# Two-layer hybrid trunk: sums of squares taken where the latents leave PSUM, negations on another engine, corner products as a stream of their own

## The chip, the cores and the metric

One core of a Trainium2 chip runs the whole program, in one launch. The metric is the device time of one execution in microseconds (us). Before the change the median of three runs is 3110.48 us (3110.13 to 3112.98).

## What is computed

Two identical layers over 1024 tokens of width 1024, all in float32. Each layer is a mixer block and a convolutional feed-forward block, each with a norm before and after. In the mixer one projection feeds four head groups:

```python
h = rms_norm(x, pre_mix_norm[l]); p = h @ w_in[l]
pa, pb, pc, pd = split_last(p, [A_COLS, B_COLS, C_COLS, D_COLS])
o = concat([mla_mixer(pa), gqa_mixer(pb), mamba2_mixer(pc), deltanet_mixer(pd)])
x = x + rms_norm(o @ w_out[l])
x = x + rms_norm(conv_ffn(rms_norm(x)))
```

Two parts matter here. Group A is latent attention: its 352 columns are a query latent of 192, a key-value latent of 128 and 32 rotary columns. Each latent is RMS-normalised over its own columns and then projected up to queries, keys and values, so each token needs two sums of squares. Group D is a gated delta rule in chunks of 64 tokens: for every chunk and head a unit lower-triangular 64 x 64 matrix is inverted. Its two 32 x 32 diagonal blocks are inverted first, and the corner of the inverse is made of products of the inverted blocks with the 32 x 32 block off the diagonal.

## The kernel before

The engines are TensorE (PE), VectorE (DVE), ScalarE (ACT), GpSimd (POOL) and SyncE (SP), which issues nearly all DMAs. Each runs its own instructions in a fixed order and stops at the first one whose input is missing. A layer runs through three stages. In the first, `step_a` (L567) projects the columns of group A, one of eight 128-token tiles at a time; the helper at L570 copies the result out of PSUM on ACT (L572), has POOL pick out gate columns (L573) and stores 352 columns to DRAM (`pa_d`). The second, the mixing stage, does everything between the projection and the output projection. The third is the output projection and the feed-forward, long runs of full-size matmuls.

The mixing stage is the one the change touches. It is written as streams, Python generators of which each step emits the instructions of one piece of work:

- `nats` (L578): projections of token-major columns. Its matmuls are L552. Columns of z leave PSUM by a tanh on ACT (L591, into a ring of three tiles `pb`) and a multiply on DVE (L592, that frees the PSUM tile); columns of group B by a copy on ACT (L586).
- `prep_a` (L1303): loads the latents back from `pa_d` twice. The first pass (L1326 to L1329) loads eight tiles through two buffers and takes the squares on ACT with an accumulated sum; DVE makes the reciprocal roots (`rstd`, L156 to L165). The second pass, per tile, loads again (L1338), transposes on PE (L1342 to L1344), splits into two parts (`lh`, ACT L133 and DVE L135), projects (L1350, L1351 for queries, L1354 for keys and values), copies out with the reciprocal root as scale (ACT L1356, L1358, L1359), rotates on POOL and stores to `qa_d` and `ka_d` (L1366, L1367).
- `d_inverse` (L910): loads the off-diagonal blocks (`ni`), negates them on ACT (L927 for one half of the partitions, read transposed, and L928 for the other), POOL copies pieces (L931), DVE inverts by 15 substitution steps (L937, L938) and block products (L946, L947). The result goes through DRAM (`u_d`, `x_d`), and `Xi` and `NX` are loaded back with 32 x 32 blocks on the partitions (L974, L975). Then the corner: 128 matmuls of 32 x 32 (L988), in eight PSUM tiles, and two copies to `Et` on ACT for each tile (L990).
- `mixer_c` (L749): the state-space mixer of group C. Its chunk states are L796 (from `X`, `bt` and `cz`), its later matmuls L825, L833, L839 and L853, some of them in the same two-buffer PSUM pool (`p1`) as the corner.
- `att` (L1371, L1122): group A's attention and then group B's. It loads one head's keys from `ka_d` (`kn`, L1395), transposes them (L507), does the same for queries (`qn`, L1388), then scores (L1139), exponentials on ACT (L1147), transposes (L507) and products with the values (L1174).
- `mixer_d` (L994): the recurrence of group D; it reads `Et` in L1034.

The order is set in two steps. A table `when` (L439) gives each stream a start and an end on an arbitrary scale, and `weave` (L1405) divides the span by the number of steps given in `mix` (L1427) and always advances the stream whose next due time is smallest. That fixes the order in which the program is written and so its priorities; the framework's scheduler then arranges the instructions of each engine by its own estimate of the timeline. Two asserts keep `mixer_d` behind the corner and attention behind `prep_a`.

Of the kernel before, what the change touches and what calls it, by code (L numbers as in the profile page):

```python
# [10 lines left out]
F32 = mybir.dt.float32  # L11
F32R = mybir.dt.float32r
I32 = mybir.dt.int32
BF16 = mybir.dt.bfloat16
AF = mybir.ActivationFunctionType
ALU = mybir.AluOpType
# [4 lines left out]
EPS = 1e-6  # L21
# [403 lines left out]
def ring(make, n):  # L425
    tiles, k = [], [0]

    def get():
        if len(tiles) < n:
            tiles.append(make())  # L430
        k[0] += 1
        return tiles[(k[0] - 1) % n]

    return get


class Mix(Trunk):
    deep = dict(y=2, th=2, sT=1, nat=2, K=1, qn=1, p=2, WO=3)
    when = dict(T=(0, 11, 0), nats=(8.58, 18.19, -719), d_prep=(6.5, 7.0, 0),  # L439
                d_inverse=(11.23, 17.34, 0), mixer_c=(16.33, 24.6, 0), prep_a=(13.24, 18.6, 0),  # L440
                att=(19.5, 47.52, 0), mixer_d=(23.21, 43.4, 0), prep_b=(22.4, 32.29, 141))
    gate_cols = (IN_DT, 8), (IN_AB, 16)
    par_at = 2
# [111 lines left out]
    def begin(self, l, P, between=None):  # L555
        w = P["w_in"][l]
        dram = lambda n, s: self.dr.tile(s, F32, name=self.nm(n), tag=n)
        self.pa_d, self.pb_d, self.z_d = dram("pa_d", [L, 352]), dram("pb_d", [L, 512]), dram("z_d", [L, 512])
        self.k_d, self.v_d, self.qT_d = dram("k_d", [L, 256]), dram("v_d", [L, 256]), dram("qT_d", [2, 4, 64, L])
        self.xs_d, self.bn_d, self.bt_d = dram("xs_d", [L, 256]), dram("bn_d", [L, 128]), dram("bt_d", [128, L])  # L560
        self.ct_d = dram("ct_d", [8, 128, 2, 128])
        self.gin = self.par([128, 8, 24], "gin")
        self.wA = self.nat_load(w, IN_A, 352, self.gate_cols, between=between)
        self.kT, self.qT = [None, None], [None, None]
        self.done = set()

    def step_a(self, i):  # L567
        nc = self.nc

        def evac(i, po):  # L570
            e = self.s2([128, 512], nm="pa")
            nc.scalar.activation(out=e[:, :376], in_=po, func=AF.Copy)  # L572
            nc.gpsimd.tensor_copy(self.gin[:, i, :], e[:, 352:376])  # L573
            nc.sync.dma_start(self.pa_d[i * 128:(i + 1) * 128, :], e[:, :352])

        self.nat_step(self.wA, i, evac)
# [333 lines left out]
    def d_inverse(self):  # L910
        nc = self.nc
        v, g = nc.vector, nc.gpsimd
# [10 lines left out]
        for b in range(2):  # L923
            ni = self.s4([128, 32, 32], nm="ni")
            nc.sync.dma_start(ni, niv[:, b, :, b, :])
            n = self.s4([128, 32, 32], nm="nn")
            nc.scalar.activation(out=n[0:64], in_=ni[0:64].rearrange("p j i -> p i j"), func=AF.Copy, scale=-1.0)  # L927
            nc.scalar.activation(out=n[64:128], in_=ni[64:128], func=AF.Copy, scale=-1.0)  # L928
            for e in range(2):
                h = slice(16 * e, 16 * e + 16)  # L930
                g.tensor_copy(nd[:, b, e], n[:, h, h])  # L931
            nn.append(n)
# [24 lines left out]
        X, T = [nd[:, b, 0] for b in range(2)], [nd[:, b, 1] for b in range(2)]  # L957
# [12 lines left out]
        NX, X = self.s4([128, 8, 4, 32], nm="NX"), self.s4([128, 8, 4, 32], nm="Xi")  # L970
        for d in range(2):
            for cc in range(2):
                o = cc * 64 + d * 32
                nc.sync.dma_start(NX[o:o + 32], self.ni_d[d, :, :, cc, d * 32:d * 32 + 32, (1 - d) * 32:(1 - d) * 32 + 32].rearrange("t h j i -> j (t h) i"))  # L974
                nc.sync.dma_start(X[o:o + 32], self.x_d[d, :, :, cc].rearrange("t h j i -> j t h i"))  # L975
        self.Et = []
        for tp in range(4):
            if tp % 2 == 0:
# [15 lines left out]
    def mixer_d(self, o_d):  # L994
        nc = self.nc
        v, g = nc.vector, nc.gpsimd
# [16 lines left out]
        def load(s):  # L1013
            wo, km, kn = rW(), rK(), rKn()
            flat = lambda ap: ap.rearrange("p h c -> p (h c)")
            for d, t, cc in place(s):
                o = t * 128 + cc * 64
                b, ra, rb, oc = own(d)
                g.memset(wo[rb, 0, d, :, d * 32:d * 32 + 32], 0.0)
                for e in range(2):  # L1020
                    nc.sync.dma_start(wo[b + e * 32:b + 32 + e * 32, 0, d, :, e * 32:e * 32 + 32], self.u_d[d, t, :, cc, e].rearrange("h j i -> j h i"))
                nc.sync.dma_start(flat(kn[tok[d]]), self.k_d[o:o + 64, :])
                nc.sync.dma_start(flat(km[tok[d], 1, d]), self.v_d[o:o + 64, :])
                nc.sync.dma_start(wo[sta[d], 1, d], self.qT_d[d, :, :, o:o + 64].rearrange("h c i -> c h i"))
                nc.sync.dma_start(flat(wo[tok[d], 1, d]), self.q_d[d, t, cc * 64:cc * 64 + 64, :])
            return wo, km, kn
# [40 lines left out]
                for t in (s // 2, (15 - s) // 2):  # L1067
                    self.d_out(t, Od[t // 4][:, t % 4], o_d)

        assert "d_inverse" in self.done  # L1070
        q = [load(0)]
        for d in range(2):
            g.memset(q[0][1][sta[d], 1, d], 0.0)
# [229 lines left out]
    def prep_a(self, l, P):  # L1303
        nc = self.nc
        v, g = nc.vector, nc.gpsimd
# [11 lines left out]
        wkv = self.s4([128, 2, 512], F32R, "wukv")  # L1317
        nc.scalar.activation(out=wkv[:, 0, :], in_=raw, func=AF.Copy, scale=self.gcol[:, 2:3])
        v.scalar_tensor_tensor(wkv[:, 1, :], raw, self.gcol[:, 2:3], wkv[:, 0, :].bitcast(F32), op0=ALU.mult, op1=ALU.subtract)
        ssq, ssk = self.t(self.sml, [128, 8], F32, "ss8"), self.t(self.sml, [128, 8], F32, "ss8")  # L1320
        rSrc, rL, rQK = (ring(lambda nm=nm, dt=dt: self.s2([128, 384], dt, nm), n) for nm, dt, n in (("pa", F32, 2), ("lh", F32R, 4), ("qa", F32, 4)))
        rJ, rTmp = ring(lambda: self.s1([128, 256]), 2), ring(lambda: self.s1([128, 4, 32]), 4)
        for t in range(8):
            junk = rJ()
            src = rSrc()[:, :352]
            nc.sync.dma_start(src, self.pa_d[t * 128:(t + 1) * 128, :])  # L1326
            nc.scalar.activation(out=junk[:, :192], in_=src[:, 0:192], func=AF.Square, accum_out=ssq[:, t:t + 1])
            junk = rJ()
            nc.scalar.activation(out=junk[:, :128], in_=src[:, 192:320], func=AF.Square, accum_out=ssk[:, t:t + 1])  # L1329
        rq = self.rstd(ssq, 1.0 / 192, EPS, 8)  # L1330
        rk = self.rstd(ssk, 1.0 / 128, EPS, 8)
        v.tensor_scalar(rq, rq, 96 ** -0.5, None, op0=ALU.mult)
        VA = []
        qa_d = self.dr.tile([L, 4, 96], F32, name=self.nm("qa_d"), tag="qa_d")
# [1 line left out]
        for t in range(8):  # L1336
            src = rSrc()[:, :352]
# [19 lines left out]
            k = rQK().rearrange("p (h c) -> p h c", h=4)  # L1357
# [69 lines left out]
    def mix(self, l, P, o_d, tail):  # L1427
        first = self.load_T(*self.T_jobs(l, P)[0][:2])
        self.params_ready()
        self.gates()  # L1430
        self.gains_ready()
        att = self.chain(self.attend_a(o_d), self.attend_b(tail))
        self.weave(T=(self.run_T(self.T_jobs(l, P), first, self.nc.gpsimd, True), 11), nats=(self.nats(l, P), 33), d_prep=(self.d_prep(), 8),
                   d_inverse=(self.d_inverse(), 25), mixer_c=(self.mixer_c(o_d), 17), prep_a=(self.prep_a(l, P), 8),
                   att=(att, 70), mixer_d=(self.mixer_d(o_d), 34), prep_b=(self.prep_b(l, P), 6))

    def out_proj(self, l, P, o_d, *tail):
# [143 lines left out]
```

## Time and profile before

| | us |
|---|---|
| median of three runs | 3110.48 |
| the profiled execution | 3117.32 |
| its span, first to last instruction | 3115.5 |
| PE busy | 2980.0 (96%) |
| DVE busy | 1814.4 (58%) |
| ACT busy | 1232.6 (40%) |
| POOL busy | 700.4 (22%) |

The profile is of one execution. Times in it are microseconds from the start of the span. "Idle before" is the time for which an engine had nothing running before an instruction, and behind the arrow stands what came last of the things it waited for. "PEclk" is the clock that TensorE was granted, as a share of 2.4 GHz; it has two levels, 1.00 and 0.50. A float32 matmul is recorded as more than one instruction, so a count of records is not a count of calls: one call of the corner product leaves two records.

### The profile page before, as it was taken

The page shows a single profiled execution, that of the slowest core. Times are in us where ns is not written, and L with a number is a line of the kernel's source. Part 1 is how long each engine was busy: PE and PEld are TensorE (multiplying, and loading weights), DVE is VectorE, ACT ScalarE, POOL GpSimd, SP SyncE. Part 2 cuts the span into 40 slices and gives each one's busy share as a digit, 9 for nine tenths or more (in the row PEclk, how much of TensorE's full clock was granted, in tenths as well). Part 3 has the DMA queues.
Part 4 walks back from the last instruction along what each step waited for, and adds up shares of the span by engine and source line. Part 5 has one row for each costly group of instructions (what it writes and reads, how often), then busy time and mean ns, then how long its engine had stood idle before and what let it go on. Part 6 is the DMA issues. An engine that isn't in the chain of part 4 may idle for free. (4 is left out here: it accounts for less than half of the span.)

```text
span 3115.5 us, 48496 instructions
## 1 busy us (share of the span) xinstructions
PE 2980.0 (96%) x18206; PEld 2437.2 (78%) x18206; DVE 1814.4 (58%) x3368; ACT 1232.6 (40%) x2607; POOL 700.4 (22%) x1173
## 2 busy tenths in 40 slices
PE   7998999999999999999899999999999999999998
PEld 7777767777888888888787777677778888888886
DVE  4555586684545555555555555866845455555556
ACT  4343346774432222222233334467734322222221
POOL 2365275321100000000133652753211000000002
PEclk9999899999999999999999998999999999999999
DMA  5255433242311111111332555333423121111212
GB/s 152 72 149 156 132 90 90 75 134 82 101 55 54 58 52 41 41 48 59 92 114 75 162 141 130 91 87 80 125 93 102 48 61 55 41 41 48 61 34 115
DMA packets 387053, 267.78 MB, mean 86 GB/s; under 512 B 148320, under 2 KB 355716, under 8 KB 386820
## 3 DMA queue, kind: packets, MB, share of 16 engines
q1 hardware_dynamic: 386820, 264.69, 29.3%
q8 instruction: 144, 2.36, 0.3%
q14 instruction: 89, 0.73, 0.1%
HBM read 195.58 MB, written 68.94 MB: 85 GB/s over the span
## 5 line engine op out<-in xcount | busy, mean ns | idle before, releaser
L263 PE MATMUL p<-hT,wh 128*128 128x512 f32 x3456 | 960.5, 392 | 6.1 <-ACT cy L388 2.6
L263 PEld LDWEIGHTS p<-hT,wh 128*128 128x128 f32 x3456 | 649.7, 189 | 143.2 <-ACT cy L388 3.4
L263 PE MATMUL p<-hT,wl 128*128 128x512 f32 x1728 | 553.0, 391 | 0.0
L263 PEld LDWEIGHTS p<-hT,wl 128*128 128x128 f32 x1728 | 325.4, 189 | 68.1 <-DVE wl L135 0.9
L388 ACT ACTIVATE cy<-p,cw 128x1024 f32<-128x1024 f32 x88 | 105.9, 1204 | 593.8 <-PE p L263 593.8
L221 POOL TENSOR_TENSOR acc<-acc,gain 128x768 f32<-128x768 f32 x12 | 24.1, 2006 | 1404.5 <-ACT junk L177 1404.4
L389 DVE SCALAR_TENSOR_TENSOR cy<-p,cw,cy 128x1023 f32<-128x1023 f32 x88 | 112.8, 1282 | 362.0 <-ACT cy L388 361.7
L552 PE MATMUL p<-wn,hT 128*128 128x256 f32 (+1 forms) x1920 | 286.6, 303 | 21.0 <-ACT hT L133 8.3
L552 PEld LDWEIGHTS p<-wn,hT 128*128 128x128 f32 x1920 | 262.6, 195 | 32.2 <-DVE pb L592 9.9
L133 ACT ACTIVATE wh<-raw 128x512 fp32r<-128x512 f32 x216 | 128.0, 623 | 182.6 <-PE p L263 93.4
L1141 DVE TENSOR_REDUCE nm<-p 128x1 f32<-128x1024 f32 x128 | 155.8, 1219 | 45.9 <-PE p L1139 45.2
L507 PE MATMUL pt<-ident,p 128*128 128x128 f32 x1024 | 152.9, 281 | 12.3 <-DVE pT L1162 5.1
L362 DVE TENSOR_TENSOR acc<-acc,p 128x512 f32<-128x512 f32 x160 | 109.7, 686 | 92.8 <-PE p L358 92.8
L1473 PE MATMUL p<-wo,oh 128*128 128x512 f32 x512 | 162.3, 395 | 0.8 <-ACT oh L133 0.8
L362 DVE TENSOR_TENSOR acc<-acc,pt 128x512 f32<-128x512 f32 x160 | 109.6, 685 | 90.7 <-PE pt L358 88.9
L1147 ACT ACTIVATE p<-p,nm 128x1024 f32<-128x1024 f32 x128 | 142.6, 1114 | 49.0 <-DVE nm L1141 33.3
L507 PEld LDWEIGHTS pt<-ident,p 128*128 128x128 f32 x1024 | 118.4, 143 | 44.2 <-issue 7.1
L135 DVE TENSOR_TENSOR wl<-raw,wh 128x512 fp32r<-128x512 f32 x180 | 116.7, 686 | 61.6 <-ACT wh L133 61.5
L358 PE MATMUL p<-owh,gh 128*128 128x512 f32 x352 | 137.8, 391 | 7.1 <-DVE acc L362 6.8
L358 PE MATMUL pt<-owh,gh 128*128 128x512 f32 x352 | 138.0, 392 | 2.1 <-DVE acc L362 2.1
L358 PE MATMUL pt<-owl,gh 128*128 128x512 f32 x352 | 137.8, 391 | 0.0
L358 PE MATMUL p<-owh,gl 128*128 128x512 f32 x352 | 137.5, 391 | 0.0
(322 smaller groups left out, 5325.4 us busy)
## 6 DMA issues: line engine op xcount, KB each, us to landing
raw<-in_f_w_in_dram SPq DMA_DIRECT2D x176, 256.0 KB, 3.2
raw<-in_f_w_out_dram SPq DMA_DIRECT2D x88, 256.0 KB, 2.6
raw<-in_w_in_dram SPq DMA_DIRECT2D x72, 256.0 KB, 2.9
raw<-in_w_out_dram SPq DMA_DIRECT2D x32, 256.0 KB, 3.0
xr<-x_mid SPq DMA_DIRECT2D x16, 512.0 KB, 6.3
x_mid<-xr SPq DMA_DIRECT2D x14, 512.0 KB, 2.9
orow<-o_d SPq DMA_DIRECT2D x48, 128.0 KB, 2.4
pa<-pa_d SPq DMA_DIRECT2D x32, 176.0 KB, 2.3
```

The source lines that it names most:

```text
L133: nc.scalar.activation(out=hi, in_=src, func=AF.Copy)
L135: (eng or nc.vector).tensor_tensor(lo, src, hi.bitcast(F32), op=ALU.subtract)
L263: nc.tensor.matmul(pm[:, h * 512:(h + 1) * 512], s[:, k % 4, :], self.h_mov(p, k, h), start=a, stop=b)
L358: nc.tensor.matmul(po, s[i // 2][:, tk], w[:, cs], start=a, stop=b)
L362: nc.vector.tensor_tensor(acc[i][:, cs], acc[i][:, cs], po, op=ALU.add)
L388: nc.scalar.activation(out=y, in_=p, func=AF.Identity, scale=w1, bias=b)
L389: nc.vector.scalar_tensor_tensor(y[:, 1:], p[:, :n - 1], w0, y[:, 1:], op0=ALU.mult, op1=ALU.add)
L507: self.nc.tensor.transpose(pt[:n, t, :], src(4 * c + t), self.ident)
L552: self.nc.tensor.matmul(po, self.h_sta(a, k, i), wt[k][b], start=(k == 0 and a == 0 and b == 0), stop=(k == 7 and a == 1))
L1141: v.reduce_max(nm, s, axis=AX.X, negate=True)
L1147: nc.scalar.activation(out=p, in_=s, func=AF.Exp, bias=nm, accum_out=rs)
L1473: nc.tensor.matmul(y[:, cs], s[k // 2][:, k % 2, :], W[k][w][:, cs], start=(k == 0 and s is oh and w == 0), stop=(k == 7 and s is ol))
```

## The change

Four edits, all in the mixing stage and the stage before it, for both layers:

1. `step_a` takes the sums of squares where the tile leaves PSUM: two ACT `Square` instructions (128 x 192 and 128 x 128, read from PSUM) into a new small tile `ssa`, for each of the 16 tiles of the two layers.
2. `prep_a` loses its first pass (16 loads, 32 ACT squares) and takes its reciprocal roots from `ssa`.
3. The eight negations (64 x 1024) of `d_inverse` go from ACT to POOL.
4. The corner products leave `d_inverse` and become a stream `d_edge` of four steps, due at 20.3 to 22.7 of the table's scale, where attention has begun (19.5). The rest of `d_inverse` keeps its pace (21 steps to 16.36, where it had 25 to 17.34).

```diff
-                d_inverse=(11.23, 17.34, 0), mixer_c=(16.33, 24.6, 0), prep_a=(13.24, 18.6, 0),
+                d_inverse=(11.23, 16.36, 0), d_edge=(20.3, 22.7, 0), mixer_c=(16.33, 24.6, 0), prep_a=(13.24, 18.6, 0),
...
+        self.ssa = self.par([128, 2, 8], "ssa")
...
             nc.gpsimd.tensor_copy(self.gin[:, i, :], e[:, 352:376])
+            for k, (o, n) in enumerate(((0, 192), (192, 128))):
+                nc.scalar.activation(out=e[:, 376:376 + n // 2].bitcast(BF16), in_=po[:, o:o + n], func=AF.Square, accum_out=self.ssa[:, k, i:i + 1])
             nc.sync.dma_start(self.pa_d[i * 128:(i + 1) * 128, :], e[:, :352])
...
-            nc.scalar.activation(out=n[0:64], in_=ni[0:64].rearrange("p j i -> p i j"), func=AF.Copy, scale=-1.0)
-            nc.scalar.activation(out=n[64:128], in_=ni[64:128], func=AF.Copy, scale=-1.0)
+            g.tensor_scalar(n[0:64], ni[0:64].rearrange("p j i -> p i j"), -1.0, None, op0=ALU.mult)
+            g.tensor_scalar(n[64:128], ni[64:128], -1.0, None, op0=ALU.mult)
...
+        self.e_src = NX, X
+
+    def d_edge(self):
+        nc = self.nc
+        assert "d_inverse" in self.done
+        NX, X = self.e_src
         self.Et = []
...
-        assert "d_inverse" in self.done
+        assert "d_edge" in self.done
...
-        for t in range(8):
-            junk = rJ()
-            src = rSrc()[:, :352]
-            nc.sync.dma_start(src, self.pa_d[t * 128:(t + 1) * 128, :])
-            nc.scalar.activation(out=junk[:, :192], in_=src[:, 0:192], func=AF.Square, accum_out=ssq[:, t:t + 1])
-            junk = rJ()
-            nc.scalar.activation(out=junk[:, :128], in_=src[:, 192:320], func=AF.Square, accum_out=ssk[:, t:t + 1])
-        rq = self.rstd(ssq, 1.0 / 192, EPS, 8)
-        rk = self.rstd(ssk, 1.0 / 128, EPS, 8)
+        rq = self.rstd(self.ssa[:, 0], 1.0 / 192, EPS, 8)
+        rk = self.rstd(self.ssa[:, 1], 1.0 / 128, EPS, 8)
...
-                   d_inverse=(self.d_inverse(), 25), mixer_c=(self.mixer_c(o_d), 17), prep_a=(self.prep_a(l, P), 8),
+                   d_inverse=(self.d_inverse(), 21), d_edge=(self.d_edge(), 4), mixer_c=(self.mixer_c(o_d), 17), prep_a=(self.prep_a(l, P), 8),
```

The scheduler moves much more than the diff shows. PE's order differs from that of before only inside the mixing stage of each layer (some 1600 instructions each); the feed-forward and the output projection keep theirs. Three places follow, all of layer 0; layer 1 has the same rows at the first and third of them. A row is an instruction with its line, its tiles (numbers tell buffers apart) and its size. The changed kernel's line numbers are 1 higher than those used in the text for `prep_a`, 3 higher from L578 to L906 and 9 higher for the corner and attention's scores.

The first place is ACT where the negations stood, ahead of the evacuations of z tiles (`pb`). Before:

```order
L1327 ACTIVATE s_394_2689,ss_392_2687<-pa_2690 128x192
L1329 ACTIVATE s_396_2693,ss_393_2688<-pa_2690 128x128
L1327 ACTIVATE s_394_2689,ss_392_2687<-pa_2695 128x192
L1329 ACTIVATE s_396_2693,ss_393_2688<-pa_2695 128x128
L927 ACTIVATE nn_2442<-ni_2440 64x1024
L928 ACTIVATE nn_2442<-ni_2440 64x1024
L591 ACTIVATE pb_2104<-p_359_2332 128x256
L591 ACTIVATE pb_2200<-p_360_2360 128x256
L133 ACTIVATE lh_2758<-pt_2754 128x256
```

Now, from the first split of a latent tile (`lh`) on; L594 is the former L591:

```order
L890 ACTIVATE R_1603<-p_311_1859 128x512
L133 ACTIVATE lh_2746<-pt_2742 128x256
L133 ACTIVATE lh_2746<-pt_2742 64x128
L594 ACTIVATE pb_2121<-p_355_2250 128x256
L594 ACTIVATE pb_2217<-p_358_2293 128x256
L594 ACTIVATE pb_2246<-p_359_2321 128x256
L594 ACTIVATE pb_2121<-p_360_2349 128x256
L594 ACTIVATE pb_2217<-p_361_2377 128x256
```

Nothing but evacuations of z stands there any more: twelve of L594 follow each other, and the first split has moved ahead of them.

The second place is PE where the latents' first transposes stand. Before, between two z tiles (`p_360`, `p_369`):

```order
L552 MATMUL p_360_2360<-wn_2056,hT_408 128x256 x2
L552 MATMUL p_360_2360<-wn_2056,hT_412 128x256
L1342 MATMUL pt_2754<-ident_66,pa_2690 128x128
L1343 MATMUL pt_2754<-ident_66,pa_2690 128x128
L1344 MATMUL pt_2754<-ident_66,pa_2690 64x128
L552 MATMUL p_369_2408<-wn_2061,hT_181 128x256 x2
L552 MATMUL p_369_2408<-wn_2061,hT_185 128x256
```

Now, among the instructions that build group D's matrices (L901, L898 before):

```order
L901 MATMUL p_312_1869<-dy_1164,dy_1002 64x64
L552 MATMUL p_355_2250<-wn_2058,hT_182 128x256 x2
L552 MATMUL p_355_2250<-wn_2058,hT_186 128x256
L552 MATMUL p_355_2250<-wn_2058,hT_182 128x256
L1343 MATMUL pt_2742<-ident_66,pa_2739 128x128
L1344 MATMUL pt_2742<-ident_66,pa_2739 128x128
L1345 MATMUL pt_2742<-ident_66,pa_2739 64x128
```

The transposes have moved about 120 instructions of PE ahead, into the first of these z tiles. Behind them come 14 of L552, the last eight of L901, and then 315 of L552 with no other work between.

The third place is PE where the first head's keys (`kn`) are transposed. Before, behind the corner (L988):

```order
L796 MATMUL p_486_3530<-X_3527,cz_3308 64x128 x2
L988 MATMUL p_488_3536<-Xi_3337,NX_3336 32x32 x16
L988 MATMUL p_489_3555<-Xi_3337,NX_3336 32x32 x16
L988 MATMUL p_491_3601<-Xi_3337,NX_3336 32x32 x16
L988 MATMUL p_492_3620<-Xi_3337,NX_3336 32x32 x16
L796 MATMUL p_496_3683<-X_3312,bt_3296 64x128 x2
L507 MATMUL pt_3888<-ident_66,kn_3884 96x128 x4
L507 MATMUL pt_3895<-ident_66,kn_3884 96x128 x4
L796 MATMUL p_497_3690<-X_3320,cz_3300 64x128 x2
L796 MATMUL p_500_3755<-X_3519,bt_3304 64x128 x2
L1388 MATMUL pt_3904<-ident_66,qn_3902 96x128 x4
```

Now, behind the last latent tile's projections (L1351, L1352 and L1355; L799 is the former L796):

```order
L1351 MATMUL pt_3638<-wuq_2691,lh_2872 128x384
L1352 MATMUL pt_3638<-wuq_2696,lh_2872 128x384
L1355 MATMUL pt_3645<-wukv_2701,lh_2871 128x512 x2
L1355 MATMUL pt_3645<-wukv_2701,lh_2872 128x512
L799 MATMUL p_495_3691<-X_3431,bt_3293 64x128 x2
L799 MATMUL p_496_3698<-X_3439,cz_3297 64x128 x2
L799 MATMUL p_497_3705<-X_3301,bt_3285 64x128 x2
L799 MATMUL p_498_3712<-X_3309,cz_3289 64x128 x2
L507 MATMUL pt_3723<-ident_66,kn_3719 96x128 x4
L507 MATMUL pt_3730<-ident_66,kn_3719 96x128 x4
L828 MATMUL p_525_3800<-cz_3297,bt_3293 128x256
L1389 MATMUL pt_3739<-ident_66,qn_3737 96x128 x4
```

Only eight instructions of L799 are left between the last projection and the transposes of `kn`; before, 68 of L552 and the whole corner stood there. The corner now comes in five pieces of 16 to 32 instructions between attention's score and transpose groups.

## Rows read from the trace of the kernel before

**Rows 1.** Busy time by stretch: layer 0's mixing stage and feed-forward (us, engines, PEclk, DMA).
```profile
60.00:720.00 660.00, 616.75 (x5120) 491.73 (x5120) 425.90 (x979) 349.91 (x777) 294.33 (x496) 0.95 0.40 110
850.00:1500.00 650.00, 648.69 (x2862) 537.04 (x2861) 350.09 (x489) 176.19 (x306) 0.00 (x0) 1.00 0.17 49
```

**Rows 2.** PE's waits, whole span: total us, times, longest.
```profile
PE p L552 <- DVE pb L592: 8.1, 6, 2.4
PE pt L1342 <- DMA pa<-pa_d: 6.5, 2, 3.5
PE p L988 <- DMA Xi<-x_d: 5.0, 2, 2.6
PE pt L507 <- DMA kn<-ka_d: 3.2, 2, 1.7
PE p L263 <- ACT wh L133: 1.8, 2, 0.9
PE p L552 <- ACT pb L586: 1.6, 2, 0.9
```

**Rows 3.** Timeline of PE, layer 0's z tiles: start, us, instruction [idle before <-releaser].
```profile
241.39 8.90 PE L552 MATMUL p<-wn,hT 128*128 128x256 f32 x72 [1.80 <-DVE pb L592]
253.74 0.33 PE L1342 MATMUL pt<-ident,pa 128*128 128x128 f32 x1 [3.45 <-DMA pa<-pa_d]
256.65 7.93 PE L552 MATMUL p<-wn,hT 128*128 128x256 f32 x48 [2.37 <-DVE pb L592]
```

**Rows 4.** Timeline of ACT, the same stretch.
```profile
239.87 0.36 ACT L1327 ACTIVATE s<-pa 128x192 f32<-128x192 f32 x1 [1.67 <-DMA pa<-pa_d]
...
252.73 1.95 ACT L927 ACTIVATE nn<-ni 64x1024 f32<-64x1024 f32 x1 [2.57 <-DMA ni<-ni_d]
...
255.76 0.66 ACT L591 ACTIVATE pb<-p 128x256 f32<-128x256 f32 x2
```

**Rows 5.** Timeline of PE from prep_a's last projection to the first scores.
```profile
346.44 0.96 PE L1354 MATMUL pt<-wukv,lh 128*128 128x512 f32 x3
...
359.66 3.52 PE L988 MATMUL p<-Xi,NX 32*32 32x32 f32 x124 [2.43 <-DMA Xi<-x_d]
...
368.55 0.69 PE L796 MATMUL p<-X,bt 128*64 128x128 f32 x4
370.92 1.94 PE L507 MATMUL pt<-ident,kn 128*96 128x128 f32 x8 [1.68 <-DMA kn<-ka_d]
...
375.92 2.08 PE L1139 MATMUL p<-kh,qh 96*128 96x512 f32 x4
...
384.45 1.63 PE L1139 MATMUL p<-kh,qh 96*128 96x512 f32 x6
```

**Rows 6.** Timeline of SP's queue in that stretch: start and us of each DMA issue.
```profile
348.70 0.38 SPq L1367 DMA_DIRECT2D ka_d<-qa  x1
...
355.65 1.39 SPq L975 DMA_DIRECT2D Xi<-x_d  x2
...
366.00 0.43 SPq L1395 DMA_DIRECT2D kn<-ka_d  x1
```

**Rows 7.** DMAs that write or read ka_d: from issue to landing.
```profile
DMA to landing us min/median/max: 2.9/3.9/4.7
```

**Rows 8.** Two stretches of low granted clock, layers 0 and 1, columns as in rows 1.
```profile
360.10:383.90 23.80, 21.90 (x304) 16.23 (x298) 10.86 (x30) 8.99 (x21) 7.94 (x12) 0.50 0.41 110
...
1909.70:1926.80 17.10, 14.71 (x293) 11.74 (x294) 5.92 (x20) 7.78 (x19) 3.68 (x6) 0.50 0.40 103
```

**Rows 9.** POOL, groups by line: busy us, mean ns | idle before, releaser.
```profile
L658 POOL TENSOR_TENSOR th<-nat,ex 128x1024 f32<-128x1024 f32 x8 | 15.3, 1913 | 11.0 <-DVE nat L645 6.7 <-PE pt L507 4.3
...
L931 POOL COPY nd<-nn 128x256 f32<-128x256 f32 x8 | 3.0, 400 | 39.2 <-ACT nn L928 39.2
```

**Rows 10.** ACT, groups by line: attention's exponentials and the corner's copies.
```profile
L1147 ACT ACTIVATE p<-p,nm 128x1024 f32<-128x1024 f32 x128 | 142.6, 1114 | 49.0 <-DVE nm L1141 33.3 <-PE pt L507 9.2 <-issue 4.1
...
L990 ACT ACTIVATE Et<-p 32x256 f32<-32x256 f32 x32 | 12.0, 375 | 11.8 <-PE p L988 11.5
```

More of the change, by code (lines that the diff above doesn't have):

```diff
@@ L1319, in prep_a @@
         v.scalar_tensor_tensor(wkv[:, 1, :], raw, self.gcol[:, 2:3], wkv[:, 0, :].bitcast(F32), op0=ALU.mult, op1=ALU.subtract)
-        ssq, ssk = self.t(self.sml, [128, 8], F32, "ss8"), self.t(self.sml, [128, 8], F32, "ss8")
         rSrc, rL, rQK = (ring(lambda nm=nm, dt=dt: self.s2([128, 384], dt, nm), n) for nm, dt, n in (("pa", F32, 2), ("lh", F32R, 4), ("qa", F32, 4)))
-        rJ, rTmp = ring(lambda: self.s1([128, 256]), 2), ring(lambda: self.s1([128, 4, 32]), 4)
-        for t in range(8):
-            junk = rJ()
-            src = rSrc()[:, :352]
-            nc.sync.dma_start(src, self.pa_d[t * 128:(t + 1) * 128, :])
-            nc.scalar.activation(out=junk[:, :192], in_=src[:, 0:192], func=AF.Square, accum_out=ssq[:, t:t + 1])
-            junk = rJ()
-            nc.scalar.activation(out=junk[:, :128], in_=src[:, 192:320], func=AF.Square, accum_out=ssk[:, t:t + 1])
-        rq = self.rstd(ssq, 1.0 / 192, EPS, 8)
-        rk = self.rstd(ssk, 1.0 / 128, EPS, 8)
+        rTmp = ring(lambda: self.s1([128, 4, 32]), 4)
+        rq = self.rstd(self.ssa[:, 0], 1.0 / 192, EPS, 8)
+        rk = self.rstd(self.ssa[:, 1], 1.0 / 128, EPS, 8)
         v.tensor_scalar(rq, rq, 96 ** -0.5, None, op0=ALU.mult)
```

## The prediction

> **What bounds it now.** I read first the busy time by stretch. In layer 0's feed-forward PE is busy 648.7 of 650 us; in the mixing stage 616.8 of 660, at a mean clock of 0.95 [rows 1]. All that can be won lies in the mixing stages, as PE's idle time and low clock. DVE, the next engine, is busy 426 of those 660 us, so it is no bound over the stage. The second view, PE's waits, says what ended that idle time; four of its rows belong to what the change touches [rows 2], and their totals are over both layers. They are the z evacuation (8.1 us), the load of the latents (6.5), the corner's input (5.0) and the first keys (3.2), together 22.8 us. The third view is the timelines around these waits.
>
> For the first two, PE loses 1.80, 3.45 and 2.37 us within 16 us of layer 0 [rows 3]. ACT shows why [rows 4]: it stands in front of a square whose load is late, and a negation waits 2.57 us for its own load, runs 1.95 us and is followed by its other half; the evacuation of z, ready long before, starts at 255.76. For the other two, PE's timeline and SP's queue go together [rows 5, 6]. The last keys are written at 348.70, but their load is issued only at 366.00, because it stands in SP's queue behind loads that wait for L796, which stands on PE behind the corner, which waited until 359.66 for a load issued at 355.65. So the corner delays the first keys.
>
> **The change, part by part.** All terms are for both layers, against the profiled execution (3117.3 us; it lies 6.8 above the median of the runs).
>
> *First pass and negations off ACT.* Twelve evacuations of z now follow each other on ACT, and the first transposes of a latent stand so early that their load has long landed. I take the z wait and the latents' wait as gone: 8.1 + 6.5 = **14.6 us**. Behind the 3.45 us wait the L552 records take 7.93/48 = 165 ns where they took 8.90/72 = 124 ns before it [rows 3]; 48 of them at the faster pace save 2.0 us, and I count the same for layer 1: **4.0 us**. The least is none of either, if another wait stands in the same place; the reciprocal roots are no candidate, since their sums now come a stage earlier.
>
> *Negations on POOL.* The trace has no negation on POOL. Four copies of 256 elements take 4 x 400 ns = 1.6 us, and a two-input operation on 1024 takes 1.9 us [rows 9]; with eight of them 13 to 15 us, all on an engine that sat idle 39.2 us before its copies waiting for ACT's halves. The substitution on DVE needs them, and it now stands behind the twelve z products. I cost them at nothing; without that cover, four of them, 6.4 to 7.7 us a layer, would pass to the inverse and from there to the corner's input.
>
> *Squares in the first stage.* The shape of 192 took 0.36 us [rows 4], the other is smaller, so 32 of them are at most 11.5 us of ACT. No wait of PE for L572 stands among its waits, so ACT keeps up there with a margin. Where ACT is late already is the split of the first weights behind this stage, 0.9 us in each layer [rows 2]; a pair of squares comes ahead of it. I put 0.5 us a layer there: **-1.0 us**, between 0 and -11.5.
>
> *Corner among attention tiles.* The waits for Xi and kn go in their old form: 5.0 + 3.2 = **8.2 us**. The corner's own PE time (256 records at 3.52/124 = 28 ns, 7.3 us a layer) is moved, not saved. The wait for a group B copy (1.6 us [rows 2]) stood between that block of L552 and the corner; L552 is now spread among the latent tiles, and I count it gone: **1.6 us**.
>
> *The new wait for the keys.* This is the dearest term. Nothing but eight L796 now lies on PE between the last projection and the transposes of kn. Before, the last projection started at 346.44 and lasted 0.96, so it ended at 347.40, and its keys were issued for writing 1.3 us later [rows 5, 6]. A write takes 2.9 to 3.9 us to land and the read that follows at most 4.7 [rows 7]: 8.9 to 9.9 us from the projection to the transposes. The eight L796 cover four groups at 0.69 or less [rows 5], some 2 us, and the loads of Xi stand just ahead of kn in the queue, which I put at 0.8 us. PE is idle 8.3 us in each layer: **-16.6 us**. The ends are 5 us (shortest landings, early read) and 13 (the queue, see the second rival).
>
> *Clock around it.* Now a stretch of 23.8 us in layer 0 and of 17.1 in layer 1 runs at half clock (0.50, that is 1.2 GHz), which begins at the wait for Xi and lasts into the first scores [rows 8]; ahead of it PE had stood still for 2.43 us, and within it for 1.68 [rows 5]. A score takes 2.08/4 = 520 ns in it and 1.63/6 = 272 ns after it [rows 5]. The longer wait will bring the clock down as well. What lies in the slow stretch afterwards is nearly the same: transposes and the first twelve scores; the L796 that stood between them now run ahead of the wait at full clock. I take **+1 us** a layer, so +2.0, between -12 and +6.
>
> Sum: 14.6 + 4.0 - 1.0 + 8.2 + 1.6 - 16.6 + 2.0 = 12.8 us. The profiled time falls to 3104.5, and the median by as much, to about **3098 us**. A difference under 0.2% (6.2 us) can't be told from none here.
>
> **Rivals.**
>
> *A shorter wait for the keys (chance 0.14).* If the write lands at its fastest and the read sooner than 4.7, PE waits 5 us rather than 8.3. For it: the 2.9 us that the fastest landing took [rows 7]; against it, that no row shows a read as short. Gain 12.8 + 6.6 = 19.4: about 3091 us.
>
> *Keys behind the corner's inputs (0.16).* SP issues in order, and kn still stands behind the two loads of Xi, which follow the store of the inverse. Xi's loads went out at 355.65 [rows 6]. The inverse now starts behind twelve z products but gets its buffers earlier. If Xi's loads go out no sooner than now, kn follows them at about 360 and the wait is near 13 us: 4.7 us more in each layer. Gain 12.8 - 9.4 = 3.4: about 3107, no difference that can be told. Against it: the L552 that free those buffers run earlier by the waits that go, some 8 us a layer in the z stretch.
>
> *The clock stays low through more of attention (0.08).* In the slow stretch now, 256 records are corner products that take about 28 ns; afterwards scores would fill it. If all of 24 us run at half clock on work that halves with it, 12 us are lost where about 6 are now: 6 us more in each layer, gain about 1, 3110 us. Against it: the stretch in layer 1 is only 17.1 us after the same waits [rows 8], so its length isn't fixed by the work. The Trainium skill has this as a rule against such a change ("TensorE: Matmul & The Clock Gate", section "HAM oscillation — how this bites in real kernels"): a burst of matmuls behind every long wait on a DMA starts throttled, so one gathered wait that reaches the throttle costs its idle time and a slow start as well. By that rule the change leaves the slow start where it was, as the traces already show one there; it speaks for the loss here only so far as dearer work stands behind the wait.
>
> *Corner groups hold attention up (0.12): slower.* The corner's eight PSUM tiles a layer come from the two buffers that L825 and L853 use, and each is emptied by a pair of copies (2 x 0.375 us) that stands on ACT behind exponentials of 1.11 us [rows 10]. If PE waits for one exponential and one pair in each case, 16 x 1.87 = 30 us are lost, and the time is about 3098 + 30 = 3128. It turns slower than before when a group costs more than 12.8/16 = 0.8 us. Against it: the order puts several score and transpose groups between two corner pieces, except where two tiles come together as one piece of 32.
>
> That the change doesn't do what it says I leave out: the order shows the moves.
>
> **How the numbers follow.** My forecast has 0.50 with a range of 3093 to 3103, all of it faster by over 6.2 us; with the shorter wait that makes 0.64, and half of the second rival's upper part adds 0.05. Within 0.2% lie the rest of the second rival and most of the third: 0.18. Slower is the fourth, with a remainder for the Squares at their upper bound: 0.13. The range of 3086 to 3112 leaves out the fourth rival and the best case of the first.
>
> **What would show it.** In the profile after: the waits of L552 for pb and of L1342's transposes for pa gone or under 1 us in all; a wait of PE's L507 on kn of 7 to 10 us in each layer, with low clock right behind it; no wait for Xi; PE's busy time in 60 to 720 us hardly changed. The prediction is wrong if the kn wait is over 12 us, if waits on the corner's copies (Et) or of L825 and L853 appear in attention with several us, or if the z stretch keeps a wait over 2 us, whose releaser would then name the negations on POOL or DVE.

## The result, and the profile after

The changed kernel takes 3139.83 us (median of five runs, 3137.54 to 3142.72) against 3111.34 us before: the ratio is 1.0082, with a 95% interval of 1.0070 to 1.0093. It is slower by 26 us by the ratio and 28 by the medians, where 13 us of gain were forecast.

The profiled execution after has a span of 3136.6 us, 21.1 more than that of before. The first view to read is again the busy time by stretch, here for layer 0's mixing stage, the whole feed-forward window of [rows 1], and 600 us of it:

```profile
60.00:720.00 660.00, 621.71 (x5161) 492.91 (x5161) 428.37 (x986) 342.46 (x755) 312.49 (x503) 0.96 0.40 108
850.00:1500.00 650.00, 650.00 (x2804) 526.74 (x2804) 339.32 (x476) 171.60 (x298) 0.00 (x0) 1.00 0.17 49
900.00:1500.00 600.00, 600.00 (x2589) 486.31 (x2588) 315.87 (x442) 152.94 (x265) 0.00 (x0) 1.00 0.16 46
```

The last of these windows before the change:

```profile
900.00:1500.00 600.00, 600.00 (x2649) 496.99 (x2648) 318.98 (x447) 155.36 (x270) 0.00 (x0) 1.00 0.16 46
```

PE is busy for all of 600 us in both, at the full granted clock (1.00), and never waits. But it starts 2649 matmuls before and 2589 after: one every 226.5 ns before, one every 231.8 ns after. Nothing in this stage was moved; PE has the same instructions in the same order there. The page's groups of the costliest instructions say which matmuls are longer. Before:

```profile
L263 PE MATMUL p<-hT,wh 128*128 128x512 f32 x3456 | 960.5, 392 | 6.1 <-ACT cy L388 2.6
L358 PE MATMUL p<-owh,gh 128*128 128x512 f32 x352 | 137.8, 391 | 7.1 <-DVE acc L362 6.8
```

After:

```profile
L263 PE MATMUL p<-hT,wh 128*128 128x512 f32 x3456 | 982.7, 398 | 6.5 <-DVE cy L390 2.5
L358 PE MATMUL p<-owh,gh 128*128 128x512 f32 x352 | 138.1, 392 | 6.4 <-DVE acc L362 6.1
```

A record of L263, the projections of the feed-forward and of the channel-major mixer columns, went from 392 to 398 ns; L358 hardly changed. PE's timeline shows it best. Before:

```profile
1000.04 1.07 PE L263 MATMUL p<-hT,wh 128*128 128x512 f32 x4
1000.95 0.62 PE L263 MATMUL p<-hT,wl 128*128 128x512 f32 x2
1001.40 1.07 PE L263 MATMUL p<-hT,wh 128*128 128x512 f32 x4
```

After:

```profile
1000.79 1.10 PE L263 MATMUL p<-hT,wh 128*128 128x512 f32 x4
1001.72 0.63 PE L263 MATMUL p<-hT,wl 128*128 128x512 f32 x2
1002.19 1.10 PE L263 MATMUL p<-hT,wh 128*128 128x512 f32 x4
```

Six matmuls take 1.36 us before (1000.04 to 1001.40) and 1.40 us after (1000.79 to 1002.19): 227 ns each became 233. There are 5184 of L263 (their operands are of the type float32r, and a call leaves one record), so an estimate for this alone is 5184 x 6.6 ns = 34 us.

Where the change meant to act, it gained. The output projection of layer 0 starts at 722.21 before and at 713.82 after; that of layer 1 at 2271.67 and 2277.20, where layer 1 itself had begun 8.4 us late, so that its mixing stage took 2.9 us less. The first row is of before, the second of after:

```profile
722.21 0.73 PE L1473 MATMUL p<-wo,oh 128*128 128x512 f32 x2 [0.40 <-ACT oh L133]
```
```profile
713.82 0.73 PE L1474 MATMUL p<-wo,oh 128*128 128x512 f32 x2 [0.40 <-ACT oh L133]
```

PE's waits after, over the whole span, against [rows 2]:

```profile
PE p L1043 <- DVE y L857: 12.9, 2, 6.6
...
PE p L799 <- DVE X L796: 5.5, 2, 2.8
...
PE p L799 <- DMA bt<-bn_d: 2.9, 2, 1.5
...
PE p L263 <- ACT wh L133: 2.4, 2, 1.2
...
PE pt L507 <- DMA kn<-ka_d: 0.9, 2, 0.7
```

The four waits of [rows 2] that the prediction spoke of (8.1, 6.5, 5.0 and 3.2 us) are gone but for 0.9 us. New are the waits of L799 and, not foreseen, 6 us in each layer in which L1043, the start of group D's recurrence, waits for a step of group C's mixer on DVE (L857). L1043 doesn't read `y`: both take PSUM tiles from the two-buffer pool `p1`, and L857 is the one that empties a tile of it. DVE comes to L857 late, behind rotations of group B (L1228), here in layer 0:

```profile
452.99 4.00 DVE L1228 TENSOR_TENSOR tmp<-raw,ropeB 128x32 f32<-128x32 f32 x4
...
461.17 0.41 DVE L857 TENSOR_TENSOR y<-y,p 128x256 f32<-128x256 f32 x1
```
```profile
461.63 0.64 PE L1043 MATMUL p<-WO,Et 32*32 32x32 f32 x16 [6.30 <-DVE y L857]
```

The place where the wait for the keys was expected, in PE's timeline after:

```profile
352.42 0.97 PE L1355 MATMUL pt<-wukv,lh 128*128 128x512 f32 x3
353.32 0.44 PE L799 MATMUL p<-X,bt 128*64 128x128 f32 x4
353.96 0.44 PE L799 MATMUL p<-X,cz 128*64 128x128 f32 x4 [0.20 <-DMA cz<-bn_d]
355.85 0.44 PE L799 MATMUL p<-X,bt 128*64 128x128 f32 x4 [1.45 <-DMA bt<-bn_d]
359.05 0.69 PE L799 MATMUL p<-X,cz 128*64 128x128 f32 x4 [2.77 <-DVE X L796]
360.48 1.91 PE L507 MATMUL pt<-ident,kn 128*96 128x128 f32 x8 [0.73 <-DMA kn<-ka_d]
```

From the end of the last projection (353.39) to the transposes of kn it is 7.1 us, of which PE stands still for 5.2 (8.3 were forecast), in four pieces. The last of them is the keys' own: kn is what the transposes wait for until 360.48. SP's queue in that stretch has the write and the read of the keys:

```profile
353.93 0.39 SPq L1368 DMA_DIRECT2D ka_d<-qa  x1
...
356.31 0.37 SPq L1396 DMA_DIRECT2D kn<-ka_d  x1
```

### The profile page after: what moved, and what is told of

Same layout as the page of the kernel before. It is cut to its first block, busy times and chain, and to the rows that moved or that the text cites. A ratio compares the mean times of both kernels' runs of the same rounds, so it can differ in the third digit from the quotient of the medians.

```text
span 3136.6 us, 48411 instructions
## 1 busy us (share of the span) xinstructions
PE 3007.8 (96%) x18206; PEld 2429.7 (77%) x18206; DVE 1810.4 (58%) x3368; ACT 1218.3 (39%) x2599; POOL 733.6 (23%) x1181
## 5 line engine op out<-in xcount | busy, mean ns | idle before, releaser
L263 PE MATMUL p<-hT,wh 128*128 128x512 f32 x3456 | 982.7, 398 | 6.5 <-DVE cy L390 2.5
L263 PEld LDWEIGHTS p<-hT,wh 128*128 128x128 f32 x3456 | 651.0, 189 | 163.5 <-issue 3.3
L263 PE MATMUL p<-hT,wl 128*128 128x512 f32 x1728 | 564.7, 397 | 0.0
L263 PEld LDWEIGHTS p<-hT,wl 128*128 128x128 f32 x1728 | 326.1, 189 | 78.1 <-DVE wl L135 0.9
L552 PE MATMUL p<-wn,hT 128*128 128x256 f32 (+1 forms) x1920 | 281.5, 300 | 12.4 <-ACT hT L133 7.2
L552 PEld LDWEIGHTS p<-wn,hT 128*128 128x128 f32 x1920 | 259.0, 193 | 22.3 <-ACT hT L133 7.8
L358 PE MATMUL p<-owh,gh 128*128 128x512 f32 x352 | 138.1, 392 | 6.4 <-DVE acc L362 6.1
L358 PE MATMUL pt<-owh,gh 128*128 128x512 f32 x352 | 138.5, 393 | 2.1 <-DVE acc L362 2.1
L358 PE MATMUL pt<-owl,gh 128*128 128x512 f32 x352 | 138.6, 394 | 0.0
L358 PE MATMUL p<-owl,gh 128*128 128x512 f32 x352 | 138.3, 393 | 0.0
```

The source lines that it names most:

```text
L263: nc.tensor.matmul(pm[:, h * 512:(h + 1) * 512], s[:, k % 4, :], self.h_mov(p, k, h), start=a, stop=b)
L358: nc.tensor.matmul(po, s[i // 2][:, tk], w[:, cs], start=a, stop=b)
L552: self.nc.tensor.matmul(po, self.h_sta(a, k, i), wt[k][b], start=(k == 0 and a == 0 and b == 0), stop=(k == 7 and a == 1))
```

## The experiments

What could have made L263 slower without moving it is its place in SBUF. The new tile `ssa` is 64 bytes a partition and is taken in `begin`, right behind `gin` (L562), ahead of the tiles of 2 KB that hold the split weights `wh` and `wl`; these are the stationary operand of L263. The moving operand `hT` is among the tiles of 4 KB, ahead of `ssa`; which of these tiles it takes changes, but its address modulo 256 stays. The compiled program gives each tile's address: modulo 256, the weights of L263 lie at 160 where they lay at 96, and `hT` lies at 96 in both. The theory is that the distance of the two operands in SBUF sets the pace. In the table a distance is the address of the weights less that of the moving operand, modulo 256 bytes; the ratio is of the runs to those of the kernel before that belong to them.

| kernel | distance, L263 | mean of L263 (hT, wh) | ratio, 95% interval |
|---|---|---|---|
| before | 0 | 392 ns | 1 |
| the change (ssa 64 bytes) | 64 | 398 ns | 1.0082 (1.0070 to 1.0093) |
| the change, ssa 128 bytes | 128 | 398 ns | 1.0085 (1.0070 to 1.0100) |
| before, weights moved by 64 | 64 | 398 ns | 1.0114 (1.0098 to 1.0131) |
| before, weights moved by 32 | 32 | 398 ns | 1.0114 (1.0099 to 1.0129) |
| before, both moved by 32 | 0 | 393 ns | 0.9984 (0.9975 to 0.9994) |
| the change, ssa behind the weights | 0 | 392 ns | 0.9958 (0.9941 to 0.9974) |
| the change, ssa 256 bytes | 0 | 392 ns | 0.9959 (0.9944 to 0.9973) |

What else lies behind `ssa` moves too. Attention's scores (L1148, 640 matmuls of 128 x 512) are at 64 in the change as well; where they follow each other they start some 2 ns later than before, about 1 us in all by an estimate from these starts.

**ssa of 128 bytes.**

```diff
-        self.ssa = self.par([128, 2, 8], "ssa")
+        self.ssa = self.par([128, 32], "ssa")[:, :16].rearrange("p (k t) -> p k t", k=2)
```

> The change with its new tile ssa made 128 bytes a partition instead of 64, so that every tile behind it lies where it lay modulo 128; the order of all engines stays that of the change. Theory A (the 64 bytes shift the weights of L263 from 96 to 32 modulo 128, and each of the 5184 matmuls then starts 6.5 ns later): the interval of L263 in the feed-forward is 227 ns again and the time is 3139.8 - 5184 x 6.5 ns - some 4 us of L358 = about 3102 us. Rival B (the slower matmuls come from the change itself, its order or its extra work): 233 ns and about 3140 us.

Measured: 3142.22 us, ratio 1.0085. The place modulo 128 was restored and nothing changed: neither the number nor the reason of theory A as put here was right. Taken alone, this run spoke for rival B; the next one decided.

**64 unused bytes in the kernel before.**

```diff
-        self.gin = self.par([128, 8, 24], "gin")
+        self.gin = self.par([128, 8 * 24 + 16], "gin")[:, :192].rearrange("p (t c) -> p t c", t=8)
```

> The kernel before with nothing changed but 64 unused bytes a partition behind the tile gin, so that the weights of L263 lie at 32 modulo 128 as in the change. Theory A: interval of L263 233 ns, mean record 398 ns, time 3111 + 34 to 38 = 3145 to 3149 us. Rival B: 227 ns and 3111 us.

Measured: 3151.28 us against 3114.89, 36 us slower with the same instructions in the same order. The window of 600 us:

```profile
900.00:1500.00 600.00, 600.00 (x2590) 486.30 (x2589) 309.23 (x433) 154.39 (x266) 0.00 (x0) 1.00 0.16 47
```

2590 matmuls, about as in the change (2589). So the place of the weights is enough, and rival B falls.

**All tiles moved by 32.** The constants' tile is made 32 bytes larger, so that everything behind it moves.

```diff
-        m = self.t(self.cst, [128, N_MASK], F32, "masks")
+        m = self.t(self.cst, [128, N_MASK + 8], F32, "masks")[:, :N_MASK]
```

> The kernel before with 32 unused bytes behind the constants, so that all large tiles, weights and moving operands both, lie at 0 modulo 128. Theory A1 (a float32 operand that starts off a 128-byte line costs TensorE time on each matmul, 96 less than 32): interval of L263 below 227 ns, towards 512 columns at 2.4 GHz = 213 ns, and the time falls by up to 5184 x 13 ns = 67 us and more with L552, L358 and L1473, to 3000 to 3050 us. Theory A2 (only the difference of the two operands' addresses matters, equal is best): 227 ns and 3111 us.

Measured: 3110.60 against 3114.89 us, 2649 matmuls in the 600 us, as before. The weights lie at 0 modulo 128 here and L263 is no faster, which speaks against A1; the distance is as before. The ratio of 0.9984 has an interval just clear of 1; a later run comes back to it.

**Only the weights moved by 32.** As the run with 64 bytes, but 8 numbers in place of 16.

```diff
-        self.gin = self.par([128, 8, 24], "gin")
+        self.gin = self.par([128, 8 * 24 + 8], "gin")[:, :192].rearrange("p (t c) -> p t c", t=8)
```

> The kernel before with 32 unused bytes behind gin: the weights of L263 at 0 modulo 128, the moving operand still at 96, as are both operands of L358, L552 and the output projection. Theory A1: L263 at or below 227 ns, the others as before, time 3111 us or less. Theory A2: the operands differ, so L263 is slower than 227 ns and the time is 3125 to 3150 us.

Measured: 3150.66 us, ratio 1.0114. These weights begin at 128 modulo 512, just as in the run before this one, which was fast; only the moving operand differs. So it is the distance of the two that counts and not where the weights lie.

```profile
900.00:1500.00 600.00, 600.00 (x2588) 485.78 (x2588) 308.63 (x432) 154.11 (x267) 0.00 (x0) 1.00 0.16 47
```

**The change, with ssa behind the weights.**

```diff
-        self.ssa = self.par([128, 2, 8], "ssa")
         self.wA = self.nat_load(w, IN_A, 352, self.gate_cols, between=between)
+        self.ssa = self.par([128, 2, 8], "ssa")
```

> The change with one line moved: ssa is taken behind the first weight tiles, so the weights of L263 lie where they lay before the change. Order of all engines as in the change. Theory A (place of the weights): interval of L263 227 ns, feed-forward as long as before, and the gain of the mixing stages is left over: 3111 - 12 to 18 = 3093 to 3103 us. Rival B (something else in the change slows the matmuls): 233 ns and about 3140 us.

Measured: 3103.12 against 3116.39 us, ratio 0.9958 (0.9941 to 0.9974), 13 us faster, with the pace of before, so rival B falls here too:

```profile
900.00:1500.00 600.00, 600.00 (x2649) 496.96 (x2648) 321.44 (x449) 152.87 (x264) 0.00 (x0) 1.00 0.15 47
```

**ssa of 256 bytes**, in its old place.

```diff
-        self.ssa = self.par([128, 2, 8], "ssa")
+        self.ssa = self.par([128, 64], "ssa")[:, :16].rearrange("p (k t) -> p k t", k=2)
```

> The change with ssa made 256 bytes a partition (it was 64, and 128 in an earlier run): the weights of L263 move by 256 bytes against before, their distance from the moving operand stays the same modulo 256. Theory A3 (the two operands must differ by a multiple of 256 bytes; shifts of 32, 64 and 128 are all slow, a shift of both together is not): 227 ns and the time of the run with ssa behind the weights, 3093 to 3103 us. Rival A4 (only the old distance, or one modulo 512 and more, is fast): 231 to 236 ns and about 3140 us.

Measured: 3103.64 us, ratio 0.9959. Here the weights did move, by 256 bytes, and the time is that of the run above. Distances of 32, 64 and 128 modulo 256 were slow, 0 is fast (before it is 256 modulo 512, here 0): A3 stands, A4 falls. Other distances were not run.

**The same for other matmuls.** 64 bytes ahead of the tiles of 1 KB, 192 more behind gin.

```diff
         load(0)
+        nc.gpsimd.memset(self.par([128, 16], "pad"), 0.0)
...
-        self.gin = self.par([128, 8, 24], "gin")
+        self.gin = self.par([128, 8 * 24 + 48], "gin")[:, :192].rearrange("p (t c) -> p t c", t=8)
```

> The kernel before with 64 unused bytes ahead of the small tiles and 192 more behind gin (and one memset of 64 bytes on POOL at the start): the operands of L263 keep their distance modulo 256, while the weights of L358 and of the output projection L1473, which lie among the small tiles, are shifted by 64 against their moving operands. If the distance is what counts, in every matmul of this kind: L263 at 227 ns, L358 and L1473 at 231 to 236 ns where they run alone, and 2112 x 6.5 ns + 768 x 6.5 ns = 19 us more, about 3135 us. If it is peculiar to the weights of L263 or to their region: 3116 us.

Measured: 3133.78 against 3116.22 us, ratio 1.0054 (1.0037 to 1.0071), 17.6 us slower, near the 19 expected. In the page's groups L263 keeps its mean, while L358 and L1473 rise (391 and 395 ns before).

```profile
L263 PE MATMUL p<-hT,wh 128*128 128x512 f32 x3456 | 962.0, 392 | 6.6 <-ACT cy L388 2.6
L1473 PE MATMUL p<-wo,oh 128*128 128x512 f32 x512 | 164.6, 399 | 0.8 <-ACT oh L133 0.8
L358 PE MATMUL p<-owh,gh 128*128 128x512 f32 x352 | 139.9, 397 | 6.4 <-DVE acc L362 6.4
```

The Trainium skill ("TensorE: Matmul & The Clock Gate", section "Step-by-step: what each phase is for") says that TensorE reads the moving operand and the weights of the next matmul through two separate ports, so that loading weights takes no read bandwidth from the running matmul. By it the place of the two should not matter; these runs show that it does, 227 against 231 to 233 ns, and the measurement decides. Why it does, and whether it is these two reads that meet, no run here shows.

**Which edit gains.** With ssa behind the weights, parts of the change were left out. Corner back at the end of the inverse (25 steps to 17.34, no stream `d_edge`):

```diff
-                d_inverse=(11.23, 16.36, 0), d_edge=(20.3, 22.7, 0), mixer_c=(16.33, 24.6, 0), prep_a=(13.24, 18.6, 0),
+                d_inverse=(11.23, 17.34, 0), mixer_c=(16.33, 24.6, 0), prep_a=(13.24, 18.6, 0),
...
         self.e_src = NX, X
+        yield from self.d_edge()
```

> As the run with ssa behind the weights, but the corner products back at the end of the inverse (25 steps to 17.34). The z evacuation and the latents' load should still have no wait (18.6 us of the forecast's sum); the waits for Xi and kn, 8.2 us over both layers, come back, and the new wait ahead of kn (5.2 us in layer 0 by the trace of the change) goes. By the forecast's sum this edit costs about 5 us, so 3090 to 3097 us; by the trace of the change it costs nothing or wins up to 4 us, so 3100 to 3107 us with the first run at 3100.

Measured: 3095.15 against 3116.39 us, ratio 0.9935 (0.9920 to 0.9950): 21 us faster than before and 8 faster than with the corner moved, and, together with the next run, the fastest of these versions. The waits for Xi and kn come back with 5.6 us. The forecast's sum, by which the corner's move loses 5 us, was nearer than the first reading of the trace after.

Negations on ACT again, corner moved:

```diff
-            g.tensor_scalar(n[0:64], ni[0:64].rearrange("p j i -> p i j"), -1.0, None, op0=ALU.mult)
-            g.tensor_scalar(n[64:128], ni[64:128], -1.0, None, op0=ALU.mult)
+            nc.scalar.activation(out=n[0:64], in_=ni[0:64].rearrange("p j i -> p i j"), func=AF.Copy, scale=-1.0)
+            nc.scalar.activation(out=n[64:128], in_=ni[64:128], func=AF.Copy, scale=-1.0)
```

> As the run with ssa behind the weights, but the negations on ACT again. If the negations in front of the z evacuations were a cause of their own, a wait of L552 for pb of 2 to 3 us comes back in each layer with some low clock: 5 to 8 us slower than with them on POOL. If the missing first pass alone removed these waits: the same time within 2 us.

Measured: 3096.81 us, ratio 0.9938 (0.9923 to 0.9953). Both expectations missed: it is faster by 6 us than with the negations on POOL. L552 waits for pb again, 1.4 us in all, but the scheduler's order has changed too. The keys' transposes now have other work around them, here in layer 1:

```profile
1891.41 1.08 PE L507 MATMUL pt<-ident,kn 128*96 128x128 f32 x8
1892.24 3.11 PE L552 MATMUL p<-wn,hT 128*128 128x256 f32 x24
1895.28 0.44 PE L799 MATMUL p<-X,bt 128*64 128x128 f32 x4
```

With the negations on POOL (ssa behind the weights), the same place of layer 1 has the wait:

```profile
1896.87 0.44 PE L799 MATMUL p<-X,bt 128*64 128x128 f32 x4 [1.58 <-DMA bt<-bn_d]
1899.79 0.70 PE L799 MATMUL p<-X,cz 128*64 128x128 f32 x4 [2.48 <-DVE X L796]
1900.73 1.49 PE L507 MATMUL pt<-ident,kn 128*96 128x128 f32 x6 [0.24 <-DMA kn<-ka_d]
```

Edits 1 and 2 alone: both of the edits above undone together.

> Edits 1 and 2 alone (sums of squares in the first stage, no first pass), ssa behind the weights; negations on ACT, corner at the end of the inverse. If the first pass alone made the waits of z and of the latents: the time of the runs with the negations on POOL and no corner stream, 3095 to 3100 us. If the negations on ACT count: 5 to 8 us above that, with L552 waiting for pb.

Measured: 3109.51 against 3116.04 us, ratio 0.9971 (0.9958 to 0.9984). L552's wait for pb is 1.3 us, that of the latents is gone: the missing first pass alone removes most of these waits, and yet the time is 10 to 11 us above the two runs before it by the ratios (0.33 and 0.36 points). Neither alternative holds: the second had the direction, but 5 to 8 us and waits for pb as the reason.

Edits 3 and 4 alone: the first pass stays, no ssa.

```diff
-        rq = self.rstd(self.ssa[:, 0], 1.0 / 192, EPS, 8)
-        rk = self.rstd(self.ssa[:, 1], 1.0 / 128, EPS, 8)
+        rq = self.rstd(ssq, 1.0 / 192, EPS, 8)
+        rk = self.rstd(ssk, 1.0 / 128, EPS, 8)
```

> Edits 3 and 4 alone: the first pass stays as it was before, without ssa. If the gain comes from the missing first pass, nothing is gained: 3110 to 3120 us, with the wait of L1342 for pa of 3 us in each layer still there. If the move of the corner were what gains, 3103 to 3108 us.

Measured: 3122.25 against 3116.04 us, ratio 1.0017 (1.0005 to 1.0029): no gain without edits 1 and 2. The wait for pa, expected with 3 us in each layer, is 1.4 us in one; that for pb is longer than before. Its waits:

```profile
PE p L1040 <- DVE y L854: 12.6, 2, 6.3
PE p L552 <- DVE pb L592: 11.0, 10, 2.4
PE pt L507 <- DMA kn<-ka_d: 5.8, 2, 3.4
```

The first of them (L1040 is L1034 of before, L1043 of the change) is in all six kernels with the corner stream (11.9 to 12.9 us), and in none of the kernels without it. So the stream of the corner brings it.

**The fastest, moved by 32.** As the kernel with the corner back, with the larger tile of constants.

> The fastest so far (edits 1 to 3, ssa behind the weights, no corner stream) with 32 unused bytes behind the constants, so that both operands of L263 and the others lie at 0 modulo 128 and keep their distance modulo 256. The run of the kernel before with the same shift lay 0.16% below before, with an interval of 0.06 to 0.25%: if that is an effect of the lines, 3090 us here; if chance, 3095 us. The interval of L263 stays 227 ns in either case.

Measured: 3098.03 us, ratio 0.9934 (0.9919 to 0.9949), the same as without the shift. Nothing of the earlier run's 0.16% shows again, though intervals of 0.15 points either way don't exclude it.

## Why the prediction was wrong

**The step that failed** is the one that gave the change's new tile no place. Under "Squares in the first stage" the prediction costed 32 instructions of ACT, -1.0 us, with a bound of -11.5, and its first paragraph took the stages that keep their order as settled: "All that can be won lies in the mixing stages". Neither asked where the 64 bytes of `ssa` lie. They moved the weights of L263 against their moving operand, and each of 5184 matmuls then starts 6 to 7 ns later, 4224 of them in the two feed-forwards, where PE hardly waits (busy 648.69 of 650 us [rows 1]) and so each nanosecond counts. The runs put this at 36 us (64 unused bytes in the kernel before) and at 1.0082 - 0.9958 = 1.2%, some 38 us, within the change. No term, bound or rival of the prediction held it. The fourth rival, at 3128 us, came within 12 us by another mechanism: no wait on the corner's copies appeared. A wait on the two buffers that the corner shares did, but behind group C's tile and only once a layer, 12.9 us in all where the rival had 30.

**What was right, and what was luck.** Without that, the change gains 13.3 us (3116.39 to 3103.12); the sum said 12.8. That they agree is luck. Of the 12.8 the sum put 6.8 on shorter idle time of PE (14.6 - 1.0 + 8.2 + 1.6 - 16.6) and 6.0 on the clock (4.0 + 2.0). The profiled executions (one each, us) show idle time unchanged and the gain in busy time:

| kernel | span | PE busy | PE idle | mean granted clock |
|---|---|---|---|---|
| before | 3115.5 | 2980.0 | 135.5 | 0.974 |
| the change, ssa behind the weights | 3105.7 | 2970.7 | 135.0 | 0.977 |
| the same, no corner stream | 3092.7 | 2968.5 | 124.2 | 0.978 |
| the same, negations on ACT | 3094.8 | 2958.3 | 136.5 | 0.983 |
| edits 1 and 2 alone | 3109.6 | 2979.3 | 130.3 | 0.974 |

So the waits that went were replaced by others as long, and the 9.3 us of busy time are the gain of this execution (with ssa of 256 bytes PE is idle for 136.0 us, in the kernel before with all tiles moved by 32 for 135.8). The terms one by one:

- z evacuation and latents (14.6 us), and the wait for a group B copy (1.6): these waits are gone in the change.
- The faster L552 (4.0 us): its busy time falls from 286.6 us before to 280.4 with ssa behind the weights.
- Squares: the first weights' wait grew from 1.8 to 2.4 us; -0.6 where -1.0 was put.
- Xi and the old wait for kn (8.2 us): gone; the 0.9 us left for kn belong to the next term.
- The new wait, -16.6 us: it is 5.5 + 2.9 + 0.9 + 0.4 (for cz) = 9.7 us over both layers. The keys' read was issued 2.4 us after their write and its transposes began 4.2 us later, where 3.9 and 4.7 were put; Xi's loads were not in the way, so the second rival fell. More than half of it stands under L799, which waits for its operand X; but the wait for the keys ended last in both layers, so X on time would not have let the transposes start sooner.
- Missing: the wait of L1043, 12.9 us. Before, PE waited 3.5 us for `y` (at L839), of which 1.6 are left.
- The clock around the keys (2.0 us): the stretch from 350 to 400 us of layer 0 has a mean clock of 0.76 before and 0.90 after (first and second row). The third rival, that it would stay low through attention, did not come.

```profile
350.00:400.00 50.00, 44.63 (x468) 34.46 (x467) 22.50 (x63) 20.61 (x41) 17.69 (x24) 0.76 0.44 119
```
```profile
350.00:400.00 50.00, 44.18 (x361) 33.36 (x361) 28.37 (x59) 24.91 (x51) 21.34 (x32) 0.90 0.37 101
```

**Open.** Added to edits 1 and 2 (0.9971), the negations on POOL bring 0.36 points and the corner stream brings 0.33, but both together only 0.13 (each ratio is known to some 0.15 points). The traces show that the scheduler writes another order for each, that the corner stream always brings the wait of L1043, and that cover for the keys' wait is there in one order (24 L552) and missing in the other. What in its estimate makes it so was not tried. By the table, what edits 1 and 2 alone lose to the better two is busy time at a lower clock for the most part, 10.8 and 21.0 us, and not idle time (6.1 us more than the one, 6.2 less than the other). Which waits bring the clock down there is not traced.

## What to carry to other kernels

Before costing a change, list the tiles it adds and what lies behind them: a tile of 64 bytes can slow a stage that it has nothing to do with. On matmuls of 128 x 512 with float32r operands that run back to back, keep weights and moving operand a multiple of 256 bytes apart in SBUF, by taking small tiles last or padding them. When a stretch is slower with PE busy all the time, count matmuls in a window before looking for waits. And when a sum comes out right, compare its parts too: here idle time and busy time had each been forecast wrong.

## What was not expected of the hardware

The time between two matmuls of 128 x 512 depends on the distance of their operands in SBUF: 227 ns at a multiple of 256 bytes, and 600 us over 2588 to 2597 records = 231 to 232 ns in feed-forward windows with L263 at 32, 64 or 128, at the same granted clock of 1.00. It does not depend on where both lie together (both moved by 32 bytes: 2649 records, as before).

L358 in the change has means of 392 to 394 ns in its groups, where they were 390 to 392 before, though its own operands kept their distance; it runs in turns with L263. By the starts in the trace of the change, the first six L358 behind L263 take 228 to 233 ns on average and those behind them 227, as all do before: the slower pace of L263 carries over into the next few matmuls. Why is not shown.
